# A column sum over 32768 rows: first loads ahead, last rows split otherwise, the very first load in two halves

## The chip, the cores and the metric

The kernel runs on one core of one Trainium2 chip. The time is in device microseconds, from one launch; for the kernel before, three runs gave a median of 630.75 us (630.24 to 630.84). A difference of 0.2%, 1.26 us, is about what a measurement of it can tell. The profiled execution is one more run; its trace gives every instruction's time from the start of the span.

## The reference

```python
grad_output = np.random.randn(32, 1024, 2048).astype(np.float32)

def reference(grad_output):
    return np.sum(grad_output, axis=(0, 1)).astype(np.float32)
```

An input of 268.4 MB, seen as 32768 rows of 2048 numbers, is added up to one row of 2048.

## The kernel before

The rows go in blocks of 8 rows to each of the 128 partitions: 1024 rows, 8.39 MB. There are 32 such blocks. 31 of them are bulk loads into `ring`, three slots in SBUF (L81). Each is one DMA, issued by SP, in which every partition gets one run of 64 KB. SP issues the first three at once; for each later one it waits until the slot is free (the semaphore `free`).

VectorE folds a block in place (L115): 4 rows are added to 4, then 2 to 2, then 1 to 1, with a drain between the steps. It raises `folded`. TensorE then multiplies the one row left, with a matrix of ones as weights, so that the partitions are summed into `acc` in PSUM (L64): four matmuls, each for one group of 32 output partitions and one quarter of the columns. The last of the four raises `free`. VectorE and TensorE each run this in a hardware loop; TensorE aligns its code ahead of it (L131).

The last block is loaded in smaller pieces, all issued once its slot is free: 4 rows, 2 rows and 1 row (L92), then the last row in a left part of 1536 columns (L102) and a right part of 512 (L103). TensorE sums these rows without a fold. Between them it sums the last folded block. VectorE moves the right quarter of `acc` out of PSUM before the last row (L162, `part`). When the left part is summed, ScalarE copies it to `resl` (L164) and itself issues its store (L166). When the right part is summed, into the PSUM tile `last`, VectorE adds `part` to it (L172) and SP issues the second store (L176). SP waits for both stores. Then the framework's closing steps follow: all engines meet twice at a barrier, and the semaphores are cleared.

At the start all engines meet at a barrier behind four small memsets of GpSimd. SP then has a NoOp and a branch (L75, L203) ahead of the first load. ScalarE needs a table for its copy; the load of the table (L164) is put directly ahead of the copy, whose wait is a part of the copy itself.

Of the kernel before, what the change touches and what calls it, by code (L numbers as in the profile page):

```python
# [7 lines left out]
P = 128  # L8
ROWS = 8
RING = 3  # L10
TAIL = (4, 2, 1)
GROUPS = 4
PIECE = 512
QUEUE = "sync"


@with_exitstack
def kernel(
    ctx: ExitStack,
    tc: tile.TileContext,  # L20
    grad_output: bass.AP,
    out: bass.AP,
):
    nc = tc.nc
    fp32 = mybir.dt.float32
    D = out.shape[-1]
    flat = grad_output.rearrange("b s d -> (b s) d")
    R = flat.shape[0]
    assert R % (P * ROWS) == 0 and D % PIECE == 0 and sum(TAIL) + 1 == ROWS
    n_bulk = R // (P * ROWS) - 1  # L30
    n_loop = n_bulk // RING
    left = D - PIECE
    J = D // PIECE
    c = PIECE // GROUPS
    G = P // GROUPS
    W = ROWS * D
    add = mybir.AluOpType.add

    io = ctx.enter_context(tc.tile_pool(name="io", bufs=1))
    psum = ctx.enter_context(  # L40
        tc.tile_pool(name="psum", bufs=1, space=bass.MemoryType.PSUM)
    )
    ring = io.tile([P, RING * W], fp32, name="ring")
    ones = io.tile([P, P], fp32, name="ones")
    zero = io.tile([P, 8], fp32, name="zero")
    part = io.tile([P, c], fp32, name="part")
    resl = io.tile([P, (J - 1) * c], fp32, name="resl")
    resr = io.tile([P, c], fp32, name="resr")

    acc = psum.tile([P, J * c], fp32, name="acc")  # L50
    last = psum.tile([P, J * c], fp32, name="last")

    sem = tc.alloc_semaphore
    full = [sem(f"full{s}") for s in range(RING)]
    tail = [sem(f"tail{k}") for k in range(len(TAIL) + 2)]
    cons, folded, free = sem("cons"), sem("folded"), sem("free")
    summed, kept, copied, stored = sem("summed"), sem("kept"), sem("copied"), sem("stored")
    load = getattr(nc, QUEUE)

    def matmuls(dst, row, j0, j1, start=False, stop=False):  # L60

        pieces = row.rearrange("p (j g x) -> p g j x", g=GROUPS, x=c)
        for g in range(GROUPS):
            ins = nc.tensor.matmul(  # L64
                dst[g * G : (g + 1) * G, : (j1 - j0) * c],
                lhsT=ones[:, :G],
                rhs=pieces[:, g, j0:j1, :],
                start=start,
                stop=stop,
                tile_position=(0, g * G),  # L70
                skip_group_check=True,
            )
        return ins

    with tc.tile_critical():  # L75

        for i in range(n_bulk):
            s = i % RING
            if i >= RING:
                load.wait_ge(free, i - RING + 1)  # L80
            load.dma_start(  # L81
                out=ring[:, s * W : (s + 1) * W],
                in_=flat[i * P * ROWS : (i + 1) * P * ROWS].rearrange(
                    "(p m) d -> p (m d)", p=P
                ),
            ).then_inc(full[s], 16)
        s = n_bulk % RING
        load.wait_ge(free, n_bulk - RING + 1)
        rows, r = [], 0
        base = n_bulk * P * ROWS  # L90
        for k, m in enumerate(TAIL):
            load.dma_start(  # L92
                out=ring[:, s * W + r * D : s * W + (r + m) * D],
                in_=flat[base + r * P : base + (r + m) * P].rearrange(
                    "(p m) d -> p (m d)", p=P
                ),
            ).then_inc(tail[k], 16)
            rows.append([ring[:, s * W + q * D : s * W + (q + 1) * D] for q in range(r, r + m)])
            r += m
        final = ring[:, s * W + r * D : s * W + (r + 1) * D]  # L100
        src = flat[base + r * P :]
        load.dma_start(out=final[:, :left], in_=src[:, :left]).then_inc(tail[-2], 16)  # L102
        load.dma_start(out=final[:, left:], in_=src[:, left:]).then_inc(tail[-1], 16)  # L103


        nc.vector.memset(ones[:], 1.0)  # L106
        nc.vector.memset(zero[:], 0.0).then_inc(cons, 1)  # L107

        def fold(s):
            nc.vector.wait_ge(full[s], 16).then_inc(full[s], -16)  # L110
            m = ROWS // 2
            while m:
                if m < ROWS // 2:
                    nc.vector.drain()
                ins = nc.vector.tensor_tensor(  # L115
                    out=ring[:, s * W : s * W + m * D],
                    in0=ring[:, s * W : s * W + m * D],
                    in1=ring[:, s * W + m * D : s * W + 2 * m * D],
                    op=add,
                )  # L120
                m //= 2
            ins.then_inc(folded, 1)

        with nc.vector.Fori(0, n_loop):
            for s in range(RING):
                fold(s)
        for i in range(n_loop * RING, n_bulk):
            fold(i % RING)


        nc.tensor.addr_align(256, max_nops=0)  # L131
        nc.tensor.wait_ge(cons, 1)
        nc.tensor.matmul(  # L133
            acc[:, : zero.shape[-1]], lhsT=ones[:], rhs=zero[:], start=True, stop=False,
            skip_group_check=True,
        )

        def sum_fold(s):
            nc.tensor.wait_ge(folded, 1).then_inc(folded, -1)  # L139
            matmuls(acc, ring[:, s * W : s * W + D], 0, J).then_inc(free, 1)  # L140

        with nc.tensor.Fori(0, n_loop):
            for s in range(RING):
                sum_fold(s)
        for k in range(len(TAIL)):
            if k == len(TAIL) - 1:
                for i in range(n_loop * RING, n_bulk):
                    sum_fold(i % RING)
            nc.tensor.wait_ge(tail[k], 16)
            for row in rows[k]:  # L150
                ins = matmuls(acc, row, 0, J)
        ins.then_inc(summed, 1)
        nc.tensor.wait_ge(tail[-2], 16)
        nc.tensor.wait_ge(kept, 1)
        matmuls(acc, final, 0, J - 1, stop=True).then_inc(summed, 1)
        nc.tensor.wait_ge(tail[-1], 16)
        matmuls(last, final, J - 1, J, start=True, stop=True).then_inc(summed, 1)


        pieces = out.rearrange("(j g x) -> g j x", g=GROUPS, x=c)  # L160
        nc.vector.wait_ge(summed, 1)
        nc.vector.tensor_copy(out=part[:], in_=acc[:, (J - 1) * c :]).then_inc(kept, 1)  # L162
        nc.scalar.wait_ge(summed, 2)
        nc.scalar.copy(out=resl[:], in_=acc[:, : (J - 1) * c]).then_inc(copied, 1)  # L164
        nc.scalar.wait_ge(copied, 1)
        nc.scalar.dma_start(  # L166
            out=pieces[:, : J - 1, :],
            in_=resl[::G, :].rearrange("g (j x) -> g j x", x=c),
        ).then_inc(stored, 16)
        nc.vector.wait_ge(kept, 1)  # L170
        nc.vector.wait_ge(summed, 3)  # L171
        nc.vector.tensor_tensor(  # L172
            out=resr[:], in0=last[:, :c], in1=part[:], op=add
        ).then_inc(cons, 1)
        nc.sync.wait_ge(cons, 2)
        nc.sync.dma_start(out=pieces[:, J - 1, :], in_=resr[::G, :]).then_inc(stored, 16)  # L176
        nc.sync.wait_ge(stored, 32)


# [28 lines left out]
```

## Time and profile before

| what | value |
|---|---|
| runs | median 630.75 us, 630.24 to 630.84 |
| profiled execution | 629.72 us |
| its span, first to last instruction | 627.9 us |
| granted TensorE clock | 1.00 |
| busy share of VectorE, TensorE | 76%, 11% |
| read from HBM | 268.44 MB, 428 GB/s over the span |
| issue to landing of a bulk load, median | 40.2 us |
| wait of VectorE for landings | 136.3 us in 31 waits |

How to read the profile: part 1 of the page gives each engine's busy time. Part 2 cuts the span into 40 slices of 15.7 us; a digit is the busy share in tenths, and the row DMA is the mean share of the core's 16 DMA engines. In the timeline, a line is start, duration, engine, line of the kernel, operation, what it writes and reads, how many, and in brackets how long the engine had been idle and what released it. SPq and ACTq are the issuing of DMAs by SP and ScalarE, PEq the instruction stream of TensorE. In the view of waits, a line is who waited for whom, microseconds in total, how often, and the longest.

### The profile page before, as it was taken

The page shows a single profiled execution, that of the slowest core. Times are in us where ns is not written, and L with a number is a line of the kernel's source. Part 1 is how long each engine was busy: PE and PEld are TensorE (multiplying, and loading weights), DVE is VectorE, ACT ScalarE, POOL GpSimd, SP SyncE. Part 2 cuts the span into 40 slices and gives each one's busy share as a digit, 9 for nine tenths or more (in the row PEclk, how much of TensorE's full clock was granted, in tenths as well). Part 3 has the DMA queues.
Part 4 walks back from the last instruction along what each step waited for, and adds up shares of the span by engine and source line. Part 5 has one row for each costly group of instructions (what it writes and reads, how often), then busy time and mean ns, then how long its engine had stood idle before and what let it go on. Part 6 is the DMA issues. An engine that isn't in the chain of part 4 may idle for free. (4 is left out here: it accounts for less than half of the span.)

```text
span 627.9 us, 1005 instructions
## 1 busy us (share of the span) xinstructions
PE 68.4 (11%) x322; PEld 9.9 (2%) x322; DVE 478.5 (76%) x97; ACT 1.8 (0%) x2; POOL 0.2 (0%) x4
## 2 busy tenths in 40 slices
PE   0011011110011110111101111001111011110116
PEld 0000000000000000000000000000000000000001
DVE  0477977778877789777797777987778877779775
ACT  0000000000000000000000000000000000000000
POOL 0000000000000000000000000000000000000000
PEclk9999999999999999999999999999999999999999
DMA  9999999999999999999999999999999999999996
GB/s 398 405 463 405 463 405 463 405 463 405 463 405 463 405 463 405 463 405 463 405 463 405 459 409 459 409 459 409 459 409 459 409 447 422 443 426 438 430 408 260
DMA packets 5209, 268.46 MB, mean 428 GB/s; under 512 B 584, under 2 KB 600, under 8 KB 856
## 3 DMA queue, kind: packets, MB, share of 16 engines
q1 hardware_dynamic: 5192, 268.44, 98.9%
q8 instruction: 1, 0.02, 0.0%
q10 hardware_dynamic: 16, 0.01, 0.0%
HBM read 268.44 MB, written 0.01 MB: 428 GB/s over the span
## 5 line engine op out<-in xcount | busy, mean ns | idle before, releaser
L115 DVE TENSOR_TENSOR ring<-ring 128x8192 f32<-128x8192 f32 (+2 forms) x93 | 477.7, 5137 | 140.9 <-DVEq L110 136.3
L64 PE MATMUL acc<-ring,ones 128*32 128x512 f32 (+1 forms) x312 | 67.6, 971 | 554.4 <-PEq L139 542.5
L64 PEld LDWEIGHTS acc<-ring,ones 128*32 128x32 f32 x312 | 9.2, 136 | 612.2 <-issue 596.6
L162 DVE COPY part<-acc 128x128 f32<-128x128 f32 x1 | 0.3, 292 | 2.8 <-PE acc L64 2.8
L164 ACT COPY resl<-acc 128x384 f32<-128x384 f32 x1 | 0.5, 478 | 621.9 <-PE acc L64 621.9
L172 DVE TENSOR_TENSOR resr<-last,part 128x128 f32<-128x128 f32 x1 | 0.3, 292 | 1.4 <-PE last L64 1.4
L164 ACT ACT_TABLE_LOAD x1 | 1.3, 1283 | 0.9 <-SPq L75 0.9
L106 DVE MEMSET ones<- 128x128 f32 x1 | 0.2, 165 | 1.0 <-SPq L75 1.0
L133 PE MATMUL acc<-zero,ones 128*128 128x8 f32 x2 | 0.6, 372 | 1.4 <-DVE zero L107 1.4
L133 PEld LDWEIGHTS acc<-zero,ones 128*128 128x128 f32 x2 | 0.5, 314 | 1.4 <-DVE zero L107 1.4
L64 PE MATMUL last<-ring,ones 128*32 128x128 f32 x8 | 0.4, 273 | 0.0
L64 PEld LDWEIGHTS last<-ring,ones 128*32 128x32 f32 x8 | 0.2, 108 | 0.5 <-DMA ring<-in_grad_output_dram 0.5
L192 POOL MEMSET const-uint8-127<- 128x1 uint8 x1 | 0.1, 102 | 0.0
L192 POOL MEMSET const-bfloat16-1.0<- 128x1 bf16 x1 | 0.1, 101 | 0.0
L192 POOL MEMSET const-float32-0.0<- 128x1 f32 x1 | 0.1, 98 | 0.2 <-issue 0.2
L192 POOL MEMSET const-float32-1.0<- 128x1 f32 x1 | 0.1, 98 | 0.0
L107 DVE MEMSET zero<- 128x8 f32 x1 | 0.1, 65 | 0.0
## 6 DMA issues: line engine op xcount, KB each, us to landing
ring<-in_grad_output_dram SPq DMA_DIRECT2D x1, 4096.0 KB, 30.6
ring<-in_grad_output_dram SPq DMA_DIRECT2D x1, 2048.0 KB, 35.1
ring<-in_grad_output_dram SPq DMA_DIRECT2D x1, 1024.0 KB, 37.1
ring<-in_grad_output_dram SPq DMA_DIRECT2D x1, 768.0 KB, 38.5
ring<-in_grad_output_dram SPq DMA_DIRECT2D x31, 40.2
ring<-in_grad_output_dram SPq DMA_DIRECT2D x1, 256.0 KB, 38.7
out_dram<-resl ACTq DMA_DIRECT2D x1, 6.0 KB
out_dram<-resr SPq DMA_DIRECT2D x1, 2.0 KB
```

Of the source, the lines that this page charges most:

```text
L64: ins = nc.tensor.matmul(dst[g * G : (g + 1) * G, : (j1 - j0) * c], lhsT=ones[:, :G], rhs=pieces[:, g, j0:j1, :], start=start, stop=stop, ...
L106: nc.vector.memset(ones[:], 1.0)
L107: nc.vector.memset(zero[:], 0.0).then_inc(cons, 1)
L115: ins = nc.vector.tensor_tensor(out=ring[:, s * W : s * W + m * D], in0=ring[:, s * W : s * W + m * D], in1=ring[:, s * W + m * D : s * W ...
L133: nc.tensor.matmul(acc[:, : zero.shape[-1]], lhsT=ones[:], rhs=zero[:], start=True, stop=False, skip_group_check=True,)
L162: nc.vector.tensor_copy(out=part[:], in_=acc[:, (J - 1) * c :]).then_inc(kept, 1)
L164: nc.scalar.copy(out=resl[:], in_=acc[:, : (J - 1) * c]).then_inc(copied, 1)
L172: nc.vector.tensor_tensor(out=resr[:], in0=last[:, :c], in1=part[:], op=add).then_inc(cons, 1)
L192: nc = _bacc.Bacc("TRN2", target_bir_lowering=False, num_devices=1)
```

## The change

The kernel is rewritten in these points:

- The first loads are issued ahead of the framework's own steps: SP and ScalarE issue them directly behind the opening barrier, and the framework is closed right behind (two barriers of all engines come there, and none at the end). The rest of the program is written out by hand, with own semaphores that are counted down by each wait, as an instruction of its own.
- The very first load is two DMAs: partitions 0 to 63 issued by SP, 64 to 127 by ScalarE, each with its own semaphore. VectorE waits for `half_in` once, ahead of its loop, and for `full[0]` in it. The bytes per partition are as before, 64 KB.
- The third add of a fold writes a buffer of its own, `sumrow`; TensorE raises `free` when it sees `folded`, and VectorE waits for TensorE (`taken`) before it writes `sumrow` again.
- 30 bulk blocks instead of 31. The last 16 rows are loaded as 7 rows (folded by VectorE), 4 rows and 3 rows (summed by TensorE), and two rows of which both left parts come first and then both right parts.
- `acc` holds the columns in another order. The right part is collected in `last`, into which VectorE copies what `acc` has of it (64 partitions, 256 columns). At the end ScalarE copies the left part (128 partitions, 512 columns), and VectorE and ScalarE each copy one half of the right part out of one partition. SP issues all three stores.
- In the built program, ScalarE's wait for `left_done` stands as an instruction of its own ahead of the table load that the copy needs.

```diff
+    early = [
+        engine.dma_start(out=slot(0, 0, ROWS)[p : p + P // 2], in_=rows[p : p + P // 2])
+        .then_inc(semaphore, 16)
+        for engine, p, semaphore in ((nc.sync, 0, full[0]), (nc.scalar, P // 2, half_in))
+    ]
+    early += [load(slot(i, 0, ROWS), ROWS, full[i]) for i in range(1, RING)]
+    for ins in early:
+        tc.no_tile_sem_insts.add(ins.ins.name)
+    nc.tensor.addr_align(256, max_nops=0)
+    tc.close()
+    tc.compile()
...
+    for i in range(RING, n_bulk):
+        nc.sync.wait_ge(free, i - RING + 1)
+        load(slot(i % RING, 0, ROWS), ROWS, full[i % RING])
...
+    load(slot(s_fold, 0, FOLD), FOLD, fold_in)
...
+    for k, m in enumerate(SINGLE):
+        load(slot(s_single, r, r + m), m, single_in[k])
...
+    for k in range(SPLIT):
+        load(split[k][:, :left], 1, left_in[k], 0, left, first_row + k * P)
+    for k in range(SPLIT):
+        load(split[k][:, left:], 1, right_in[k], left, D, first_row + k * P)
...
+    def wait(engine, semaphore, value):
+
+        engine.wait_ge(semaphore, value).then_inc(semaphore, -value)
...
+    def to_sumrow(s):
+        nc.vector.drain()
+        wait(nc.vector, taken, 1)
+        plus(sumrow[:], slot(s, 0, 1), slot(s, 1, 2)).then_inc(folded, 1)
+
+    wait(nc.vector, half_in, 16)
+    with nc.vector.Fori(0, n_bulk // RING):
+        for s in range(RING):
+            wait(nc.vector, full[s], 16)
+            plus(slot(s, 0, 4), slot(s, 0, 4), slot(s, 4, 8))
+            nc.vector.drain()
+            plus(slot(s, 0, 2), slot(s, 0, 2), slot(s, 2, 4))
+            to_sumrow(s)
...
+    with nc.tensor.Fori(0, n_bulk):
+        wait(nc.tensor, folded, 1)
+        nc.tensor.sem_inc(free, 1)
+        sum_row(sumrow).then_inc(taken, 1)
...
+    for k in range(SPLIT):
+        wait(nc.tensor, left_in[k], 16)
+        ins = sum_row(split[k], whole=False, stop=k == SPLIT - 1)
+    ins.then_inc(left_done, 1)
+    for k in range(SPLIT):
+        wait(nc.tensor, right_in[k], 16)
+        for g in range(2):
+            col = left + g * HALF
+            ins = matmul(
+                last[g * G : (g + 1) * G, :HALF], split[k][:, col : col + HALF], g,
+                stop=k == SPLIT - 1,
+            )
+    ins.then_inc(right_done, 2)
...
+    wait(nc.vector, summed, 1)
+    nc.vector.tensor_copy(out=last[: 2 * G, :HALF], in_=acc[: 2 * G, HALF:]).then_inc(kept, 1)
+    wait(nc.vector, right_done, 1)
+    nc.vector.tensor_copy(out=resr[:1, :HALF], in_=last[:1, :HALF]).then_inc(right_res, 1)
+
+    wait(nc.scalar, left_done, 1)
+    nc.scalar.copy(out=resl[:], in_=acc[:]).then_inc(left_res, 1)
+    wait(nc.scalar, right_done, 1)
+    nc.scalar.copy(out=resr[:1, HALF:], in_=last[G : G + 1, :HALF]).then_inc(right_res, 1)
+
+    wait(nc.sync, left_res, 1)
+    dst = out.rearrange("(g x) -> g x", x=HALF)
+    nc.sync.dma_start(out=dst[:2], in_=resl[: 2 * G : G, :HALF]).then_inc(stored, 16)
+    dst = out.rearrange("(g x) -> g x", x=N)
+    nc.sync.dma_start(out=dst[1:3], in_=resl[2 * G :: G, :]).then_inc(stored, 16)
+    wait(nc.sync, right_res, 2)
+    dst = out.rearrange("(g x) -> g x", x=RIGHT)
+    nc.sync.dma_start(out=dst[D // RIGHT - 1 :], in_=resr[:1, :]).then_inc(stored, 16)
+    wait(nc.sync, stored, 48)
```

The helper `load` issues one DMA on SP for the next `m` rows of each partition, `slot` names rows of a ring slot, and `sum_row` gives the four matmuls of one row.

## The prediction

> **What bounds the kernel now.** I read the page's first two parts, then the groups by shape, the timeline of VectorE's first and last stretch, SP's waits, and the timeline of the last six microseconds.
>
> ```profile
> span 627.9 us, 1005 instructions
> ...
> PE 68.4 (11%) x322; PEld 9.9 (2%) x322; DVE 478.5 (76%) x97; ACT 1.8 (0%) x2; POOL 0.2 (0%) x4
> ...
> DMA  9999999999999999999999999999999999999996
> ```
>
> No engine computes all the time, but the DMA share is 9 in every slice up to the last. The kernel is one stream of loads; all else lies beside it.
>
> ```profile
> 23.77 15.56 DVE L115 TENSOR_TENSOR ring<-ring 128x8192 f32<-128x8192 f32 x3 [22.55 <-DVEq L110]
> 39.45 0.23 PEld L64 LDWEIGHTS acc<-ring,ones 128*32 128x32 f32 x8 [37.54 <-issue]
> 39.48 1.94 PE L64 MATMUL acc<-ring,ones 128*32 128x512 f32 x8 [37.48 <-PEq L139]
> 43.13 15.56 DVE L115 TENSOR_TENSOR ring<-ring 128x8192 f32<-128x8192 f32 x3 [3.80 <-DVEq L110]
> ```
>
> Each fold starts when its load has landed: 23.77, 43.13, and the last at 604.29. That is (604.29 - 23.77) / 30 = 19.35 us a load. A fold takes 15.56, so VectorE waits 3.8 each time, and TensorE's 1.94 follow. With three slots, two loads are under way or queued whenever a slot comes free; the stream never stops. The page counts 128 large packets per load; over 16 DMA engines that is 8 each, 19.35 / 8 = **2.42 us per 64 KB packet**. So the time is: first issue (0.95), delay until data run (23.77 - 19.35 - 0.95 = 3.5), the stream, and what follows the last landing.
>
> ```profile
> SPq L176 <- DVE resr L172: 39.2, 1, 39.2
> SPq L75 <- DMA out_dram<-resr: 1.2, 1, 1.2
> ```
> ```profile
> 623.83 0.40 PE L64 MATMUL last<-ring,ones 128*32 128x128 f32 x8
> 624.08 0.48 ACT L164 COPY resl<-acc 128x384 f32<-128x384 f32 x1 [621.89 <-PE acc L64]
> 624.38 0.29 DVE L172 TENSOR_TENSOR resr<-last,part 128x128 f32<-128x128 f32 x1 [1.38 <-PE last L64]
> 624.59 1.11 ACTq L166 DMA_DIRECT2D out_dram<-resl  x1
> 624.69 0.64 SPq L176 DMA_DIRECT2D out_dram<-resr  x1
> ```
>
> The last load releases TensorE at 623.8 (call that T). The last store is issued at 624.69, takes 0.64 to issue and is waited for 1.2 more: landed at about 626.55, 1.86 after issue began. From there to 627.9 the engines only meet in the closing barriers: 1.35 us. The tail is thus T + 4.1.
>
> **The change, part by part.**
>
> 1. First issue. SP leaves the opening barrier at 0.7 (its wait of 0.7 for PEq) and then runs a NoOp and a branch before the load at 0.95. Both are gone from ahead of it: **-0.23**. Behind the early loads stand two further barriers, but they have 19 us of transfer above them; nothing is needed from VectorE before the first landing.
>
> 2. The first load in halves. ACT's queue holds nothing else then, and SP's next two loads follow its half. The bytes are the same; the question is the pace. The trace shows no load into fewer than 128 partitions, so I bound it. Lower end: every packet keeps 2.42 us, extra 0. Upper end: in a 128-partition load the 16 DMA engines have 8 partitions each; with 64 partitions they have 4 each, and if the 2.42 belongs to the place that is written and not to the DMA engine, two engines share what one had, and each packet takes 4.84. Two halves together help only where one of such a pair is on the lower half while the other is on the upper. But both queues fill at the same moment (both issuers leave the same barrier), I suppose that every DMA engine takes them in the same turn; a pair that starts together ends together: eight packets of 4.84 = 38.7 instead of 19.35, **+19.35**. A pair that starts a time d apart saves d in each packet, eight times; the slowest pair sets the end, so I take d = 0.1 and +18.5. Which end? The one row that bears on whether the pace is the DMA engine's own is the instruction packet on queue q8:
>
> ```profile
> q8 instruction: 1, 0.02, 0.2%
> ```
>
> (the DMA view of the first 40 us: 0.2% of 16 x 40 us = 1.28 us for 16 KB). At a load's pace it would need 2.42 / 4 = 0.6. [...] It is a weak row (the packet ran while everything started), but it is nearer to the upper end: **+18.5**.
>
> [...]
>
> 3. Bulk loads: the third add now goes to sumrow after a wait for `taken`; behind it on VectorE stand all later folds. PE raises it 1.94 us after the fold's end, 13 us before the next third add: hidden. A slot comes free 2 us earlier; two loads were queued anyway: 0. The new wait for `half_in` stands ahead of all folds; if the first fold is late, slot 0 is free by 41 + 16 = 57 us, while loads two and three run until about 80: still no gap.
>
> 4. Smaller last loads. From issue to landing in the trace, the pieces of 4, 2, 1, 0.75 and 0.25 rows land at 613.9, 618.75, 621.2, 623.1, 623.8: together 19.5 for 19.35. The new last 16 rows have seven pieces for the six of the old ones: **+0.1**.
>
> 5. The tail. Last landing T. The left part of the last row lands two right pieces earlier, T - 1.3 (each 623.8 - 623.1, some 0.64). TensorE's left step took 0.85 plus 0.1 until ACT was released; a control instruction is now ahead of it, and the step before may run late: left_done at T - 0.1. Now ACT. Before, its table load ran at 0.90, while nothing was needed:
>
> ```profile
> 0.90 1.28 ACT L164 ACT_TABLE_LOAD   x1 [0.90 <-SPq L75]
> ```
>
> In the changed program the wait for left_done is an instruction of its own ahead of the table load, so its 1.28 falls into the tail: T + 1.25. Copy of 512 columns, 0.48 to 0.64 from the 384-column row, taken 0.6: T + 1.85. Then SP, which now issues all three stores in a row: steps between 0.45 (its first loads are issued 0.95 to 2.29, three in 1.34) and 0.64, taken 0.45: third one at T + 2.8, though its own data (two copies of one partition) are ready by T + 2.3. Landing 1.2 to 1.86 after, taken 1.8: T + 4.6, and no closing barrier. The old tail was T + 4.1: **+0.5**.
>
> [...]
>
> **Sum** against the profiled execution (629.72 us, span 627.9): -0.23 + 18.5 + 0.1 + 0.5 = +18.9, so 648.6. The median of the runs is 1.03 above the profiled one; I keep that: **649.6**. Unknown: the slowest pair's d from 0 to 0.9 (+19.35 to +12), tail -0.8 to +0.8: own range 643 to 650.8.
>
> **Rivals.**
>
> - The halves cost nothing: the DMA engines mix both queues, or the pace is theirs. For it: nothing in the trace contradicts 2.42 per engine. Then only the small terms stay: -0.23 + 0.1 + 0.5 = +0.4, **631.1**, not slower beyond 0.2%. This ends on the other side; it decides at the first packets: with 2.42 there it holds, and only from a lengthening of 0.16 us a packet on (8 x 0.16 = 1.3) does it fail. Range 630.0 to 632.0; on its low edge, with the table load still early, 629.8.
> - The pairs fall out of step midway: once one engine of a pair ends early, it moves to the other half and both run alone. With half of the packets doubled: 4 x 2.42 = 9.7, so **640.8** (633 to 645). For it: DMA engines don't start at one moment. Against: equal sharing keeps an offset as it is.
> - That the change doesn't do what it says, the ACT half being issued late (its store at L166 took 1.11 to issue): the first fold starts later, but 3.8 us of slack a load hide it, and the time is the first rival's.
>
> **Chances.** Crowded halves 0.50, out of step 0.17, no cost 0.33 (of that 0.27 within 0.2%, which is 1.26 us and about what a measurement can tell from no change; 0.03 each side). Faster 0.03, same 0.27, slower 0.70. As no cost has more than 0.2, the range reaches to it: 630.2 to 650.8.
>
> **What would show it.** Right: the first fold starts near 42, the first two slices show about half of the GB/s, the second load is folded near 61, and from then on 19.35 a load. Wrong: the first fold starts near 23.5. For the tail: the table load after the last landing, SP's three stores within 1 us, the third landing near T + 4.6; wrong if the load stands at the start or the stores take 0.64 each.

## The result, and the profile after

The changed kernel takes **650.35 us**, the median of 5 runs (649.91 to 650.52), where the kernel before took 630.56 on the same chip (5 runs, 629.63 to 630.84). The ratio is 1.0317, with a 95% interval of 1.0305 to 1.0328: slower by 3.2%. The profiled execution is the one of 649.91 us.

From the page of the changed kernel: its span, the DMA and bandwidth rows of part 2, and two rows of the queues in part 3 (packets, MB, share of 16 engines' span).

```profile
span 648.6 us, 1130 instructions
...
DMA  9989999999999999999999999999999999999995
GB/s 199 251 263 453 449 396 449 453 408 432 453 449 392 453 449 400 445 453 420 420 453 449 392 453 449 408 437 453 441 400 453 449 392 453 453 408 432 457 396 247
...
q1 hardware_dynamic: 5274, 264.25, 95.9%
q10 hardware_dynamic: 80, 4.19, 3.0%
```

Read the two rows of part 2 together. The DMA share alone tells nothing: it is 8 or 9 from the first slice on. Beside it the first three slices, some 49 us, move 199 to 263 GB/s, and each slice behind them 392 to 457, but for the last. The DMA engines are as busy as ever and move about half. Part 3 says the same in one line: queue q10 is ScalarE's half of the first load. It has 4.19 MB, 1.6% of the bytes, and takes 3.0% of the engines' time.

The timeline of the changed kernel up to 90 us shows where it is lost:

```profile
0.73 0.58 SPq L94 DMA_DIRECT2D ring<-in_grad_output_dram  x1
0.73 0.54 ACTq L94 DMA_DIRECT2D ring<-in_grad_output_dram  x1
...
43.64 13.20 DVE L130 TENSOR_TENSOR ring<-ring 128x8192 f32<-128x8192 f32 x2 [38.64 <-DVEq L71]
...
62.55 13.19 DVE L130 TENSOR_TENSOR ring<-ring 128x8192 f32<-128x8192 f32 x2 [3.23 <-DVEq L71]
...
81.90 8.69 DVE L130 TENSOR_TENSOR ring<-ring 128x8192 f32<-128x8192 f32 x1 [3.68 <-DVEq L71]
```

Both halves are issued at 0.73, at one moment. The first fold starts at 43.64, where that of before started at 23.77. The third starts 19.35 behind the second, which is the old pace of a load. So one load is slow, the halved one, and nothing else. (The second fold starts 18.9 behind the first, since the first two landings, at 43.5 and 62.41, lie that much closer.)

The same kernel in five windows of 10 us. The columns that matter are the last three: granted clock, share of the DMA engines, GB/s.

```profile
2.00:12.00 10.00, 3.09 (x4) 0.79 (x4) 0.65 (x2) 0.00 (x0) 0.00 (x0) 1.00 1.21 262
12.00:22.00 10.00, 0.00 (x0) 0.00 (x0) 0.00 (x0) 0.00 (x0) 0.00 (x0) 1.00 1.10 236
22.00:32.00 10.00, 0.00 (x0) 0.00 (x0) 0.00 (x0) 0.00 (x0) 0.00 (x0) 1.00 1.07 229
32.00:42.00 10.00, 0.00 (x0) 0.00 (x0) 0.00 (x0) 0.00 (x0) 0.00 (x0) 1.00 0.82 210
42.00:52.00 10.00, 0.00 (x0) 0.00 (x0) 8.36 (x1) 0.00 (x0) 0.00 (x0) 1.00 0.97 419
```

In the kernel before, the same windows move 388, 452, 472, 433 and 419 GB/s. Two of them:

```profile
12.00:22.00 10.00, 0.00 (x0) 0.00 (x0) 0.00 (x0) 0.00 (x0) 0.00 (x0) 1.00 1.04 452
22.00:32.00 10.00, 0.00 (x0) 0.00 (x0) 8.23 (x1) 0.00 (x0) 0.00 (x0) 1.00 1.09 472
```

Here it is about half until 42 us, and 419 in both from then on. The share is 0.82 to 1.21 throughout.

The trace also has every packet of the DMA engines, with queue, start, length and size, but not its engine. By their starts and ends the packets form 16 chains, and each chain is taken here for one DMA engine. Times of landing are those of the last of the counts (16 for a load) with which a DMA raises its semaphore in the trace. In the kernel before, the 64 KB packets of the loads take 2.42 us, but for the first 16 (2.4 to 3.4). In the changed kernel all 16 DMA engines first take one packet of q10, then one of q1, then q10 again, in strict turns, eight rounds. The first round takes 4.1 to 5.2 us, each later one **4.88 to 4.92** (a few packets of the last one up to 4.98). The first round of the second load takes 2.7 to 3.5, and from then on it is 2.42 again.

The last five microseconds of the changed kernel, by the timeline:

```profile
643.36 0.63 PE L163 MATMUL last<-ring,ones 128*32 128x256 f32 x4
644.05 1.28 ACT L215 ACT_TABLE_LOAD   x1 [644.05 <-ACTq L71]
644.18 0.41 DVE L212 COPY resr<-last 1x256 f32<-1x256 f32 x1 [2.48 <-ACTq L71]
645.35 0.59 ACT L215 COPY resl<-acc 128x512 f32<-128x512 f32 x1
645.96 0.36 ACT L217 COPY resr<-last 1x256 f32<-1x256 f32 x1
646.02 0.62 SPq L221 DMA_DIRECT2D out_dram<-resl  x1
646.69 0.48 SPq L223 DMA_DIRECT2D out_dram<-resl  x1
647.29 0.34 SPq L226 DMA_DIRECT2D out_dram<-resr  x1
```

The last load lands at T = 643.23. The table load starts 0.82 later and holds up the copy, and with it all three stores. The third is issued at T + 4.06 and lands at 648.54, T + 5.3. Before, the end came at T + 4.17.

### The profile page after: what moved, and what is told of

The parts are those of the page before. It is cut to its first block, busy times and chain, and to the rows that moved or that the text cites. A ratio compares the mean times of both kernels' runs of the same rounds, so it can differ in the third digit from the quotient of the medians.

```text
span 648.6 us, 1130 instructions
## 1 busy us (share of the span) xinstructions
PE 72.0 (11%) x332; PEld 11.1 (2%) x332; DVE 477.2 (74%) x98; ACT 2.2 (0%) x3; POOL 0.2 (0%) x4
## 3 DMA queue, kind: packets, MB, share of 16 engines
q10 hardware_dynamic: 80, 4.19, 3.0%
## 5 line engine op out<-in xcount | busy, mean ns | idle before, releaser
L130 DVE TENSOR_TENSOR ring<-ring 128x8192 f32<-128x8192 f32 (+3 forms) x63 | 404.6, 6423 | 148.5 <-DVEq L71 146.2
L163 PE MATMUL acc<-sumrow,ones 128*32 128x512 f32 x248 | 59.1, 1042 | 556.0 <-PEq L71 556.0
L130 DVE TENSOR_TENSOR sumrow<-ring 128x2048 f32<-128x2048 f32 x31 | 71.1, 2293 | 5.8 <-DVEq L71 5.8
L163 PEld LDWEIGHTS acc<-sumrow,ones 128*32 128x32 f32 x248 | 7.2, 139 | 607.5 <-issue 607.5
L163 PE MATMUL acc<-ring,ones 128*32 128x512 f32 (+1 forms) x72 | 9.9, 667 | 10.9 <-PEq L71 10.9
L163 PEld LDWEIGHTS acc<-ring,ones 128*32 128x32 f32 x72 | 2.7, 123 | 18.6 <-issue 18.5
L156 PE MATMUL acc<-zero,ones 128*128 128x512 f32 x2 | 2.1, 1142 | 0.0
```

Source lines behind the costliest of these rows:

```text
L130: return nc.vector.tensor_tensor(out=dst, in0=a, in1=b, op=add)
L156: ins = nc.tensor.matmul(dst[:m, :n], lhsT=ones[:, :m], rhs=zero[:, :n], start=True, stop=False, skip_group_check=True,)
L163: return nc.tensor.matmul(dst, lhsT=ones[:, :G], rhs=rhs, start=False, stop=stop, tile_position=(0, g * G), skip_group_check=True,)
```

## The experiments

**Theory**, called crowding in the expectations: the pace belongs to the places in SBUF that are written, and when all 16 DMA engines write into partitions 0 to 63, or into 64 to 127, two of them share what one has in an undivided load. The strict turns bring them to the same half at about the same time, so each packet takes twice 2.42 us. The sharing is my supposition: the packets show the doubling, 4.88 to 4.92, and not what makes it. **Rivals:** it is two queues taking turns that costs; or two DMAs in place of one; or that each DMA has only 64 partitions, whichever these are; or the loss comes from another part of the rewrite.

Experiment 2 starts from the kernel before. In 1 and in 3 to 10 only the first load of the changed kernel is issued otherwise, and VectorE waits for all its pieces; 11 and 12 start from experiment 1. Times are medians with their range, or a single execution where that is said. Packet lengths come from the trace's packet records.

**1. The first load undivided, all else as changed.**

```diff
-        engine.dma_start(out=slot(0, 0, ROWS)[p : p + P // 2], in_=rows[p : p + P // 2])
-        .then_inc(semaphore, 16)
-        for engine, p, semaphore in ((nc.sync, 0, full[0]), (nc.scalar, P // 2, half_in))
+        nc.sync.dma_start(out=slot(0, 0, ROWS)[0:128], in_=rows[0:128]).then_inc(full[0], 16),
```

> The changed kernel with its first load as one DMA of 128 partitions again, issued by SP; all else as changed. [...] In the trace the second load lands at 62.41 us in the changed kernel and at 43.00 before; with the issue 0.22 earlier it would land at 42.8, so 19.6 less: 630.7 to 631.6 us, the first packets at 2.4 to 3.4 us. Rival (the loss lies elsewhere, in the early issue or in the new tail): stays above 640.

Measured: 630.30 us (630.08 to 630.47), a ratio of 0.9999 (0.9990 to 1.0008) to the kernel before. VectorE's first fold in its timeline:

```profile
23.47 13.20 DVE L127 TENSOR_TENSOR ring<-ring 128x8192 f32<-128x8192 f32 x2 [19.78 <-DVEq L71]
```

Packets take 2.42 us, and the second load lands at 42.70 where the changed kernel has 62.41: 19.7 us. The whole loss goes with the division. The rest of the rewrite together makes no difference that can be measured; 630.7 to 631.6 had been expected.

**2. The kernel before with the division alone.**

```diff
+            if i == 0:
+                load.dma_start(out=dst[: P // 2], in_=src[: P // 2]).then_inc(full[s], 16)
+                nc.scalar.dma_start(out=dst[P // 2 :], in_=src[P // 2 :]).then_inc(half_in, 16)
+                continue
...
+        nc.vector.wait_ge(half_in, 16).then_inc(half_in, -16)
```

> The kernel before with one edit: its first load is issued as partitions 0 to 63 by SP and 64 to 127 by ScalarE, and VectorE waits for both. Crowding: 8 packets of 4.89 instead of 2.42, and the somewhat long first packets of before are hidden in it: +19.2 to +19.8, so 649.8 to 650.4 us. Rival (the loss needs the rest of the rewrite, such as the early issue): near 630.6.

Measured: 649.72 us (649.26 to 650.42), ratio 1.0315 (1.0299 to 1.0331). The first fold in its timeline, with the three adds of the old fold:

```profile
43.70 15.56 DVE L119 TENSOR_TENSOR ring<-ring 128x8192 f32<-128x8192 f32 x3 [42.48 <-DVEq L114]
```

The division alone is enough to make the loss, with none of the rewrite around it, and nearly all packets behind the first round take 4.88 to 4.90. Experiments 1 and 2 together settle where the time goes; the next ones are about why.

**3. Both halves on SP's queue.**

```diff
+        nc.sync.dma_start(out=slot(0, 0, ROWS)[0:64], in_=rows[0:64]).then_inc(full[0], 16),
+        nc.sync.dma_start(out=slot(0, 0, ROWS)[64:128], in_=rows[64:128]).then_inc(more_in[0], 16),
```

> The changed kernel with both halves issued by SP, one behind the other, so that no DMA engine alternates between two queues. Crowding: the four packets of the lower half and then the four of the upper half take 4.89 each, 650.0 to 650.7 us as changed. Rival (two queues in turn on one DMA engine halve its pace): 2.42 a packet, near 631.

Measured: 651.47 us (651.06 to 651.65), ratio 1.0340 (1.0324 to 1.0356); first fold at 44.60. The packets of the lower half come first, then those of the upper. Nearly all take 5.12 us; the first of each half are shorter (4.2 to 5.2, and 4.93 to 5.01). So one queue loses as much, and two queues taking turns are not the cause. It is 1.1 us worse than with two; why 5.12 and not 4.89 is left open.

**4. Two DMAs on two queues, each with all 128 partitions and half of the rows.**

```diff
+        nc.sync.dma_start(out=slot(0, 0, 4)[0:128], in_=rows[0:128, 0 * D : 4 * D]).then_inc(full[0], 16),
+        nc.scalar.dma_start(out=slot(0, 4, 8)[0:128], in_=rows[0:128, 4 * D : 8 * D]).then_inc(more_in[0], 16),
```

> The changed kernel with the first load split between SP and ScalarE by rows and not by partitions: each DMA has all 128 partitions and 4 of the 8 rows, 32 KB a partition. [...] Rival (two queues in turn halve the pace): 2.42 us for 32 KB, 650.

Measured: 630.43 us (630.23 to 630.64), ratio 1.0004 (0.9995 to 1.0014). First fold:

```profile
23.74 13.20 DVE L129 TENSOR_TENSOR ring<-ring 128x8192 f32<-128x8192 f32 x2 [18.73 <-DVEq L71]
```

Again q10 and q1 take strict turns on each DMA engine, now with 32 KB packets of 1.21 us, half of 2.42. That is what I had expected from crowding, 1.21 and a time near 631, since each of the two DMAs writes all 128 partitions. Two queues in turns and two DMAs cost nothing here by themselves.

**5. Even and odd partitions.** SP loads partitions 0, 2, 4 and so on, ScalarE the odd ones: 64 partitions in each DMA as in the change, but spread over all 128.

```diff
+        nc.sync.dma_start(out=slot(0, 0, ROWS)[0:128:2], in_=rows[0:128:2]).then_inc(full[0], 16),
+        nc.scalar.dma_start(out=slot(0, 0, ROWS)[1:128:2], in_=rows[1:128:2]).then_inc(more_in[0], 16),
```

> The changed kernel with the halves made of the even partitions (SP) and the odd ones (ScalarE). [...]

Measured (one execution): 630.65 us, beside 630.01 for the kernel before on that chip. The windows of this kernel:

```profile
2.00:12.00 10.00, 3.09 (x4) 0.79 (x4) 0.65 (x2) 0.00 (x0) 0.00 (x0) 1.00 1.03 419
12.00:22.00 10.00, 0.00 (x0) 0.00 (x0) 0.00 (x0) 0.00 (x0) 0.00 (x0) 1.00 0.98 426
```

Packets of 2.42 in strict turns: full pace. **My expectation failed here.** I had expected 4.89 us a packet and 650 us, from a supposition on which partitions each DMA engine is dealt and which of them share a place; 2.42 and 631 stood against it. No run shows how the partitions are dealt. What the run does show is worth more: a DMA of 64 partitions isn't slow as such. It depends on which 64: 2.42 us a packet here, 5.12 for 0 to 63 in experiment 3.

**6. The middle half first.** Partitions 32 to 95 in one DMA of SP, then 0 to 31 on SP, and 96 to 127 on ScalarE.

```diff
+        nc.sync.dma_start(out=slot(0, 0, ROWS)[32:96], in_=rows[32:96]).then_inc(full[0], 16),
+        nc.sync.dma_start(out=slot(0, 0, ROWS)[0:32], in_=rows[0:32]).then_inc(more_in[0], 16),
+        nc.scalar.dma_start(out=slot(0, 0, ROWS)[96:128], in_=rows[96:128]).then_inc(more_in[1], 16),
```

> The changed kernel with the first load in three DMAs: partitions 32 to 95 and then 0 to 31 on SP, 96 to 127 on ScalarE. [...] Sum 4 x 2.42 + 4 x 4.89 = 29.2 instead of 39.1: 640.5 us. Rival (a DMA of 64 partitions runs at half pace whichever they are): four packets of 4.89, landing near 22 us, 650 or more in all.

Measured (one execution): 648.25 us. The windows of this kernel:

```profile
2.00:12.00 10.00, 0.00 (x0) 0.00 (x0) 0.00 (x0) 0.00 (x0) 0.00 (x0) 1.00 0.78 170
12.00:22.00 10.00, 3.09 (x4) 0.79 (x4) 0.65 (x2) 0.00 (x0) 0.00 (x0) 1.00 0.92 367
22.00:32.00 10.00, 0.00 (x0) 0.00 (x0) 0.00 (x0) 0.00 (x0) 0.00 (x0) 1.00 1.01 210
32.00:42.00 10.00, 0.00 (x0) 0.00 (x0) 0.00 (x0) 0.00 (x0) 0.00 (x0) 1.00 1.06 301
```

By the packet records ScalarE's quarter goes in the first 12 us (two rounds of 4.5 to 5.6), then the middle half in four rounds of 2.8 to 3.5, about 2.5 (one packet 4.23), 2.44 and 2.42, then the quarter 0 to 31 in two rounds of 4.6 to 5.1. This is so on 15 of the 16 engines. They take both packets of ScalarE's queue before the first of SP's, though both DMAs were issued at 0.7, so here the two queues were not served in turns. The sum rests on two estimates of mine, 2.42 us a packet for the middle half and 4.89 for the two quarters. They held roughly: the 64 neighbours 32 to 95 come down to 2.42, and the quarters take 4.5 to 5.6. The time was missed by 8 us. Slow first rounds are part of it. The rest is odd: the first round of the **second** load, with all 128 partitions, takes 5.1 too, and its second 3.1 to 3.5. One DMA engine had been held up early by the 16 KB instruction packet (2.2 us) and was still writing into the slow quarter then. Whether that held up the others, no run shows.

**7. Eight pieces of 16 neighbouring partitions**, all on SP, 0 to 15, 16 to 31 and so on.

```diff
+        nc.sync.dma_start(out=slot(0, 0, ROWS)[0:16], in_=rows[0:16]).then_inc(full[0], 16),
+        nc.sync.dma_start(out=slot(0, 0, ROWS)[16:32], in_=rows[16:32]).then_inc(more_in[0], 16),
...
+        nc.sync.dma_start(out=slot(0, 0, ROWS)[112:128], in_=rows[112:128]).then_inc(more_in[6], 16),
```

> The changed kernel with the first load in eight DMAs of 16 partitions, all on SP. [...] Rival (a split costs a factor of two, however fine it is): 650.

Measured (one execution): 684.63 us. The first fold:

```profile
78.36 13.20 DVE L135 TENSOR_TENSOR ring<-ring 128x8192 f32<-128x8192 f32 x2 [70.09 <-DVEq L71]
```

Packets of 9.23 us, 3.8 times 2.42. My estimate was four times 2.42, 9.7 us a packet and 688 us in all. A load issued as one stretch of 128 neighbours, as two of 64 (experiment 3) and as eight of 16 takes 2.42, 5.12 and 9.23 us a packet. By the rival, that it is only the division, this would have ended at 650.

One rival runs along with all of these experiments: partition p always gets the p-th 64 KB of the input, so the places that are read change with the places that are written. The kernel before speaks against it. Its load of one row reads 1 MB in one stretch, as each of these eight pieces does, but writes 8 KB to each of 128 partitions. Its packets take 0.31 to 0.32 us; an eighth of 2.42 is 0.30, an eighth of 9.23 would be 1.15. So a stretch of 1 MB of the input isn't slow to read there.

**8 and 9. The same eight pieces of 16 partitions, chosen otherwise.** In experiment 8 each piece takes every eighth partition of all 128, in experiment 9 every fourth partition of one half.

```diff
+        nc.sync.dma_start(out=slot(0, 0, ROWS)[0:128:8], in_=rows[0:128:8]).then_inc(full[0], 16),
+        nc.sync.dma_start(out=slot(0, 0, ROWS)[1:128:8], in_=rows[1:128:8]).then_inc(more_in[0], 16),
...
+        nc.sync.dma_start(out=slot(0, 0, ROWS)[7:128:8], in_=rows[7:128:8]).then_inc(more_in[6], 16),
```

> The changed kernel with the first load in eight DMAs of 16 partitions, each with every eighth partition (0, 8, ... 120 first), all on SP; every DMA engine then has one packet of each. [...] If only the spread over both sides of partition 64 counts: 2.42, 631 us. [...]

```diff
+        nc.sync.dma_start(out=slot(0, 0, ROWS)[0:64:4], in_=rows[0:64:4]).then_inc(full[0], 16),
...
+        nc.sync.dma_start(out=slot(0, 0, ROWS)[67:128:4], in_=rows[67:128:4]).then_inc(more_in[6], 16),
```

> The changed kernel with the first load in eight DMAs of 16 partitions that lie on one side of partition 64, four apart (0, 4, ... 60 first), all on SP. [...] If the number of partitions in a DMA counts and not their places: 685 as with 16 neighbours (684.6). If the side does not count: 631.

Measured (one execution each): 651.37 and 650.95 us, with packets of mostly 5.10 and 5.09. For both I had expected 4.84 us a packet and 650 us, if two DMA engines share a place; that was a supposition on which partitions share one. VectorE's first fold, in experiment 8:

```profile
45.11 13.20 DVE L135 TENSOR_TENSOR ring<-ring 128x8192 f32<-128x8192 f32 x2 [35.82 <-DVEq L71]
```

and in experiment 9:

```profile
44.38 13.20 DVE L135 TENSOR_TENSOR ring<-ring 128x8192 f32<-128x8192 f32 x2 [35.15 <-DVEq L71]
```

A DMA of 16 partitions has 16 packets of 64 KB for the 16 DMA engines, and between 12 and 42 us their busy share is 0.96 to 1.01 in both, so it isn't that the packets went to a few of them. The number of pieces and of partitions is that of experiment 7, and the packets take a bit more than half of its 9.23. So it is the choice of partitions that counts: 16 neighbours go at about a quarter of the full pace (9.23 us for 2.42), 16 spread ones in either of these patterns at half (5.10 and 5.09). What makes these sets differ, no run shows.

**10. A stretch shifted by 16**, to see whether some of the DMA engines run ahead: partitions 16 to 79, then 0 to 15, then 80 to 127, all on SP.

```diff
+        nc.sync.dma_start(out=slot(0, 0, ROWS)[16:80], in_=rows[16:80]).then_inc(full[0], 16),
+        nc.sync.dma_start(out=slot(0, 0, ROWS)[0:16], in_=rows[0:16]).then_inc(more_in[0], 16),
+        nc.sync.dma_start(out=slot(0, 0, ROWS)[80:128], in_=rows[80:128]).then_inc(more_in[1], 16),
```

> The changed kernel with the first load as partitions 16 to 79, then 0 to 15, then 80 to 127, all on SP. [...] Whole time between 640 and 655.

Measured (one execution): 665.08 us, over the range that was expected. The windows of this kernel from 12 us:

```profile
12.00:22.00 10.00, 0.00 (x0) 0.00 (x0) 0.00 (x0) 0.00 (x0) 0.00 (x0) 1.00 0.90 184
22.00:32.00 10.00, 0.00 (x0) 0.00 (x0) 0.00 (x0) 0.00 (x0) 0.00 (x0) 1.00 1.60 197
32.00:42.00 10.00, 0.00 (x0) 0.00 (x0) 0.00 (x0) 0.00 (x0) 0.00 (x0) 1.00 0.94 118
```

I had expected eight fast and eight slow engines in the first piece, 2.42 and 4.89 us a packet, again from a supposition on the dealing. All 16 take the same, 4.4 to 5.2 in the first round and then 5.12 (one packet 5.29). The sixteen neighbours 0 to 15 take 8.5 to 9.3, and the 48 partitions of the last piece 7.9 to 8.5 in each of three rounds. The simple picture, that each pair shares its place and the others run free, is not what these packets show: in each piece all 16 kept about one pace. What makes them do so stays open, as does the dealing.

**11. The undivided load, and the table load out of the tail.** Here ScalarE's wait for `left_done` becomes a part of the copy, and the count is taken down behind it.

```diff
-    wait(nc.scalar, left_done, 1)
+    nc.scalar.wait_ge(left_done, 1)
     nc.scalar.copy(out=resl[:], in_=acc[:]).then_inc(left_res, 1)
+    wait(nc.scalar, left_done, 1)
```

> The changed kernel with an undivided first load and ScalarE's wait made a part of the copy again, so that the table load can run at the start. Theory of the tail (the table load is on the path to the last store): the 1.28 us go, 630.3 of the undivided kernel less 1.3 = 629.0 us, the table load near 1 us, the last store issued 1.3 us earlier. Rival (another wait ends last, as the 4.04 us from the last landing to the third store's issue is held by SP's row of stores): under 0.4 us gained.

Measured: **628.96 us** (628.49 to 629.33), ratio 0.9981 (0.9972 to 0.9990) to the kernel before. ScalarE's timeline and the last store:

```profile
2.88 1.28 ACT L211 ACT_TABLE_LOAD   x1 [2.88 <-PEq L100]
624.00 0.59 ACT L211 COPY resl<-acc 128x512 f32<-128x512 f32 x1 [619.84 <-PE acc L159]
```
```profile
625.94 0.34 SPq L223 DMA_DIRECT2D out_dram<-resr  x1
```

The table load runs at 2.88, under the first load. In experiment 1, alike but for this, it stands at 624.30 and the last store is issued at 627.53:

```profile
624.30 1.28 ACT L211 ACT_TABLE_LOAD   x1 [624.30 <-ACTq L71]
...
627.53 0.34 SPq L222 DMA_DIRECT2D out_dram<-resr  x1
```

The medians differ by 1.34 us, on two chips, and the ratios by 0.0018, which is 1.1 us; the table load is 1.28. All runs of this version lie below all of the kernel before on the same chip (median 629.93, 629.41 to 631.09), but the gain over it, 0.97 us, is under 0.2%.

**12. The same with two shorter steps in the tail:** VectorE copies both right halves in one copy over 64 partitions, and ScalarE issues one store.

```diff
+    nc.vector.tensor_copy(out=resr[: 2 * G, :HALF], in_=last[: 2 * G, :HALF])
...
+    nc.scalar.copy(out=resl[:], in_=acc[:]).then_inc(left_res, 2)
...
+    nc.scalar.dma_start(out=dst[1:3], in_=resl[2 * G :: G, :]).then_inc(stored, 16)
```

> The same with three more edits of the tail: VectorE copies both halves of the right part in one instruction of 64 partitions, ScalarE issues one of the stores of the left part itself, and SP issues the other two. The theory of the tail: the last store is issued some 2.2 us after the last landing instead of 4.04 and lands 1.25 later: 630.3 - 1.9 = 628.4 us, below the kernel before as well. Rival (stores issued at the same time by two engines hinder each other, as before, where they took 1.11 and 0.64 us): 629.0, no gain over the early table load alone.

Measured: 630.01 us (629.70 to 630.35), ratio 0.9998 (0.9989 to 1.0007): missed. Its tail:

```profile
624.31 1.28 ACT L211 ACT_TABLE_LOAD   x1 [624.31 <-PE acc L159]
...
625.61 0.59 ACT L211 COPY resl<-acc 128x512 f32<-128x512 f32 x1
626.28 0.60 SPq L219 DMA_DIRECT2D out_dram<-resl  x1
626.30 1.29 ACTq L214 DMA_DIRECT2D out_dram<-resl  x1
627.00 0.49 SPq L221 DMA_DIRECT2D out_dram<-resr  x1
```

In the built program the wait stood again as an instruction of its own ahead of the table load (in the trace at 624.26), and so the load is back at 624.31. The copy now counts its semaphore up by 2 and not by 1; whether that is why the wait was put apart I have not tried. From the end of the copy to the last landing it took 2.34 us, where experiment 11 took 2.59: the new stores gain 0.25, and the table load takes 1.28 away.

## Why the prediction was right, step by step

| the first load as | most packets, us | first fold at | time, us |
|---|---|---|---|
| one DMA (experiment 1) | 2.42 | 23.47 | 630.30 |
| two halves, two queues (the change) | 4.88 to 4.92 | 43.64 | 650.35 |
| two halves, one queue (3) | 5.12 | 44.60 | 651.47 |
| by rows, two queues (4) | 1.21, of 32 KB | 23.74 | 630.43 |
| even and odd, two queues (5) | 2.42 | 23.61 | 630.65 |
| eight of 16 neighbours (7) | 9.23 | 78.36 | 684.63 |
| eight of every eighth (8) | 5.10 | 45.11 | 651.37 |
| eight of every fourth in a half (9) | 5.09 | 44.38 | 650.95 |

**Step 1, the first issue: right.** It went from 0.95 to 0.73, as forecast.

**Step 2, the halves: right, a little small.** Forecast were packets near 4.84 and +18.5; the packets take about 4.9, and the second load lands 19.7 us later than with an undivided one. What failed is the discount: I supposed that a pair of DMA engines that starts d apart saves d in each packet. The starts do lie up to 1.8 us apart and stay so, and no engine gains from it: one that starts 0.5 behind the others still takes 4.88. Full doubling, +19.35, was the better value. That two DMA engines then share what one had, no run shows; the runs show the doubled packets. The 38.7 us of the upper end, eight packets of 4.84, were 40.3, from the start of its first packet (2.06) to the end of its last (42.36). Choosing the upper end was right, but the weak row on which the choice rested (the 16 KB instruction packet at less than half of a load's pace) was no reason for it. That packet takes 1.19 us beside the undivided load of experiment 1 and 1.24 in the changed kernel, so its length doesn't tell the halved load from the undivided one. So far as the choice rested on it, it was luck.

**Step 3, the waits `taken` and `half_in`: nothing, right.** From the second landing to the last it takes 643.23 - 62.41 = 580.82 us, before 623.76 - 43.00 = 580.76.

**Step 4, the smaller last loads: right.** The 0.06 by which these two numbers differ holds this term together with step 3; +0.1 was forecast.

**Step 5, the tail: the mis-sized term.** Forecast was T + 4.6, it was T + 5.3. The table load fell into the tail as said, but `left_done` was not raised at T - 0.1. The left part of the last row had landed at 641.96, T - 1.3 as forecast. TensorE came late: before it adds the split rows to `acc` it waits until VectorE has copied out of it (`kept`), which the forecast had only as "the step before may run late".

```profile
641.28 0.42 DVE L210 COPY last<-acc 64x256 f32<-64x256 f32 x1 [6.37 <-DVEq L71]
...
642.01 1.06 PE L163 MATMUL acc<-ring,ones 128*32 128x256 f32 x12 [0.90 <-PEq L71]
...
643.33 0.60 PE L163 MATMUL acc<-ring,ones 128*32 128x512 f32 x2
```

So the split rows begin only at 642.01, the last left matmuls start at 643.33 and end about 643.9, and the table load starts at T + 0.82. From there to the issue of the third store it is 3.2 us, for 1.28 + 0.6 + 0.95 = 2.8 in the forecast: SP's first store took 0.62, near the 0.64 that the forecast named as a sign of being wrong. The landing took 1.25 from issue, for 1.8. So the tail costs +1.1 for the +0.5 of the forecast.

**The sum.** One term was left out. Around the span lay 629.72 - 627.9 = 1.8 us before, and 649.91 - 648.6 = 1.3 in the changed kernel. Experiment 2, which keeps the old closing steps, has 649.26 - 647.5 = 1.8, experiment 1 has 630.14 - 628.8 = 1.3. So 0.5 goes with the rewrite, whose framework steps experiment 2 doesn't have; which of them it is, no run shows. Worked out again: the second landing 62.41 - 43.00 = +19.4 (the earlier issue is in it), +0.06, the tail +1.1, around the span -0.5, together +20.1. The profiled executions differ by 20.2; the forecast was 18.9. That the time came nearer than its terms is luck: the forecast added 1.03 us from the profiled execution to the median, which in the changed kernel is 0.44 (650.35 - 649.91). So 649.6 misses 650.35 by 0.75, and that lies 0.45 inside the upper end of the range.

**The rivals.** That the halves cost nothing is what happens with even and odd partitions (630.65) or by rows (630.43), so it was the choice of partitions that decided, not the division. That the pairs fall out of step is refuted by the rounds: the seven behind the first are alike, 4.88 to 4.98. That ScalarE's half comes late is refuted by the two issues at 0.73.

## What to carry to other kernels

Don't cut a load at partition 64, on one queue or two: here it took the packets of all 16 DMA engines from 2.42 us to 4.88 to 4.92 on two queues and to 5.12 on one, for as long as these DMAs ran. If a load has to be divided, divide it along the rows (630.43 us here), or in even and odd partitions (630.65), and then compare the length of a packet, or the row of GB/s beside the DMA share, with that of the undivided load, as the share alone was 8 or 9 in the slow slices of the changed kernel too. Look also at where ScalarE's table load stands: the wait as an instruction of its own ahead of it put 1.28 us into the tail (experiment 1, load at 624.30), the wait as a part of the copy did not (experiment 11, load at 2.88).

## What the runs showed of the hardware that was not expected

- A DMA of 64 partitions runs at full pace (2.42 us for 64 KB) over the even partitions, nearly so over 32 to 95 (2.42 to 2.54 behind the first round, but for a few packets), and at half pace over 0 to 63 (5.12 on one queue).
- Two queues were served in strict turns by each DMA engine, one packet each, in the changed kernel and in experiments 2, 4 and 5, at no cost in itself (experiment 4, 1.21 us for 32 KB); in experiment 6 they were not.
- The 16 DMA engines kept one common pace in the shifted piece of experiment 10 too (5.12 us on all 16), where I had looked for fast and slow ones.
- ScalarE took 1.29 us to issue a store in experiment 12, where SP took 0.60 and 0.49 beside it; its half of the first load took it 0.54 in the changed kernel.
- A copy starts 0.02 us behind the end of the table load that it needs (644.05 + 1.28 and 645.35, in the changed kernel).
